# adaLN shift and scale made 128 features at a time with stationary weights, and the first projections of token tile 0 accumulated k-outer

## The chip, the cores and the metric

The kernel runs on all 8 cores of one Trainium2 chip, one batch element per core, with no traffic between the cores. The metric is the device time of the slowest core, in microseconds. Some executions here fell in a second, slower state, in which the cores of a die show a lower granted TensorE clock: in two slow runs of the kernel before (3706.1 and 3710.7 us) one die had 0.81. In the fast profile of the kernel before, all 8 cores were granted 1.00 in the MLP stretch (2000 to 2200 us), with PE busy 199 us or more. A profile is one execution, and the page shows its slowest core. Where I give medians over the cores, I read the same landmark on all 8 cores of the profiled execution.

## The reference, cut to what matters

```python
cond = jax.nn.silu(c)
mod = cond @ w_mod[l] + b_mod[l]                      # (B, 6D), D = 2048
sh_a, sc_a, gt_a, sh_m, sc_m, gt_m = split(mod, 6)
h = rmsnorm(x, g_pre_mix[l]) * (1.0 + sc_a) + sh_a    # (B, S, D), S = 2048
proj = h @ w_in[l]                                    # q, k, v, forget gate, ...
log_f = log_sigmoid(fg + b_forget)                    # then a cumulative sum over S
# ... forgetting attention, sliding-window attention, out projection, MLP ...
```

Only the opening is at issue: shift `sh_a` and scale `sc_a`, `h`, and the first projections (q and k of head 0, v of heads 0 and 1, and the forget gate). Nothing can be projected before the shift and scale are known, and those need 33.5 MB of fp32 weights per core.

## The kernel before: the parts that matter

Tokens are handled in 4 tiles of 512 (`t`), features in 16 groups of 128 (`k`). x lies transposed: features on partitions. Every operation names what it reads and writes; a small scheduler adds the semaphore waits. Each engine is given its own operations in program order. Weights are loaded by the POOL queue with a cast from fp32 to bf16; x and small tensors are loaded by the SP queue.

```python
R1 = Ring(P, "ra", [B[f"ring{i}"] for i in range(5)], src1, ...)   # 5 slots of 128 x 2048

def mod_slot(g, k):          # feature group k of c stationary (32 columns), 4 x 512 weights moving
    s = R1.acq(("M", g, k)); b = R1.bufs[s]
    mms = [mm(banks[MB](0, 512, p=(32*c, 32*c+32)), condpad(k), b(slice(c*512, c*512+512)), k == 0, k == KC-1)
           for c in range(4)]
    ...                      # R1.rel(s) then asks for the next slot
def mod_finish(g, pend): ... # copy to SBUF, select and transpose with 4 fp32 matmuls, add the bias

def n_stat(t, q):            # squares of 4 feature groups on ACT, summed over features by PE
    act(sqA(), x(slice(4*q, 4*q+4)), AF.Square)
    bk = banks[SB[t % 2]]
    pe([mm(bk(), ones(), sqA(i), ...) for i in range(4)], [ones(), sqA()], [bk()])
def n_z(t, k):               # x * scale * rstd, on DVE, in place
    stt(x(k), x(k), Av(0, slice(k, k+1)), rstd[t % 2](), ALU.mult, ALU.mult)
def n_h(t, k):               # + shift, to bf16
    if k % 2 == 0: act(hT(t, k), x(k), AF.Identity, bias=modT(slice(k, k+1)))
    else:          ts(hT(t, k), x(k), modT(slice(k, k+1)), ALU.add, eng="pool")

for k in range(KC):
    mod_slot(1, k)                                  # scale: 16 slots
    if k in (8, 10, 12, 14): n_stat(0, (k-8)//2)
n_rstd(0); mod_finish(1, pend0); x_load(1, extra=[o_sc]); pend0.pop(0)()
for k in range(KC):
    mod_slot(0, k); n_z(0, k)                       # shift: 16 slots
    if k in (12, 13, 14, 15): n_stat(1, k-12)
n_rstd(1); mod_finish(0, pend0); pend0.pop(0)()
for k in range(KC): n_h(0, k)
# [cut] q0, k0, v0 weights acquired from R1
for t in range(NT):          # q, k, forget gate, v of tile t; between their groups, for tile t+1:
    # n_stat x4 (t+1 >= 2), n_rstd, then n_z and n_h for 16 k; then x_load(t+2)
    ...
    fg_tr(t)                 # PE transposes of the gate's running sum; the next tile's projections follow
```

## Time and profile before

| what (core 0, the slowest) | us |
|---|---|
| whole time, median of 3 runs | 3192.5 |
| modulation weights on their way | 1.6 to about 128 |
| h of tile 0 made | 141 to 163 |
| forget-gate scan of tiles 0, 1, 2, 3 starts | 175.5, 212.4, 248.0, 267.8 |
| first forgetting-attention subtraction | 284.3 |
| everything after it | 2911 |

The four scans are good landmarks: each follows the forget-gate projection of its tile.

First the windows view of the kernel before. Each line is a stretch of 20 us: length, then the busy time and instruction count of PE, PE's weight loads, DVE, ACT and POOL, then the granted TensorE clock, the DMA engines' busy share, and GB/s.

```profile
60.00:80.00 20.00, 9.18 (x40) 3.48 (x40) 5.90 (x11) 4.37 (x4) 3.17 (x6) 0.50 1.04 189
100.00:120.00 20.00, 3.71 (x24) 0.84 (x24) 0.00 (x0) 0.00 (x0) 3.17 (x6) 0.50 1.05 178
140.00:160.00 20.00, 4.40 (x12) 1.45 (x11) 9.89 (x17) 7.38 (x12) 18.86 (x7) 0.50 0.27 46
160.00:180.00 20.00, 18.47 (x96) 9.82 (x98) 4.38 (x5) 5.06 (x8) 15.24 (x10) 0.78 0.04 9
```

In 60:80 and 100:120 the DMA engines are full and no other engine is busy half of the time. (GB/s counts what lands; the weights halve on landing, a slot of 1.049 MB landing as 512 KB, so the 178 GB/s that landed in 100:120, nearly all of it weights, are about 345 GB/s read.) From 140 to 160 us the DMA engines are nearly done, PE works 4.4 of 20 us, and POOL is busy for 18.9 us.

The timeline of the kernel before, DVE and POOL around that stretch (start, duration, engine, line, operation, destination and source, count, and the idle time before it with what ended it):

```profile
141.14 21.79 POOL L415 TENSOR_SCALAR hT<-xst_50,modT 128x512 bf16<-128x512 f32 x8 [4.36 <-DVE modT L404]
141.50 9.22 DVE L409 SCALAR_TENSOR_TENSOR xstA<-xstA,Av,rstd_81 128x512 f32<-128x512 f32 x14
175.54 1.21 DVE L696 TENSOR_TENSOR_SCAN Cf<-rr,lf 8x512 f32<-8x512 f32 x1 [2.16 <-ACT lf L401]
```

POOL takes 21.8 us for eight additions, and PE waits for them (17.4 us in 5 waits, from 0 to 290 us). What this line hides is in the tile view of the same POOL operations, which gives the shortest, median and longest of the eight in ns:

```profile
L415 POOL TENSOR_SCALAR hT<-xst_50,modT x8: 1552/1552/11010, 141.1 to 161.4; 128x512 bf16<-128x512 f32 x8
```

One takes 11.0 us, the others 1.55 us. The long one is the first, at 141.1 us, and it ends 1.4 us after DVE's run of 14 back-to-back multiplications beside it.

### The profile page before, as it was taken

The page shows a single profiled execution, that of the slowest core. Times are in us where ns is not written, and L with a number is a line of the kernel's source. Part 1 is how long each engine was busy: PE and PEld are TensorE (multiplying, and loading weights), DVE is VectorE, ACT ScalarE, POOL GpSimd, SP SyncE. Part 2 cuts the span into 40 slices and gives each one's busy share as a digit, 9 for nine tenths or more (in the row PEclk, how much of TensorE's full clock was granted, in tenths as well). Part 3 has the DMA queues.
Part 4 walks back from the last instruction along what each step waited for, and adds up shares of the span by engine and source line. Part 5 has one row for each costly group of instructions (what it writes and reads, how often), then busy time and mean ns, then how long its engine had stood idle before and what let it go on. Part 6 is the DMA issues. An engine that isn't in the chain of part 4 may idle for free.

```text
span 3195.4 us, 36955 instructions; the slowest of 8 cores (3178.6 to 3195.4 us)
## 1 busy us (share of the span) xinstructions
PE 2873.5 (90%) x13961; PEld 1359.6 (43%) x14224; DVE 876.0 (27%) x1344; ACT 757.9 (24%) x1228; POOL 585.2 (18%) x682
## 2 busy tenths in 40 slices
PE   2278988998888898999999999999999999999994
PEld 0034533666433343344444444444444444444441
DVE  0223334244444455643111100000133211000005
ACT  1142233264445434533111100000111111000000
POOL 1342133100000155530000011111100000111114
PEclk8578999999999998999999999999999999999997
DMA  9834545522333833354444455555688644444455
GB/s 190 162 106 90 86 80 83 93 50 55 67 65 76 139 106 119 139 132 70 75 79 74 79 94 97 97 95 90 139 186 194 116 73 79 74 78 76 76 95 201
DMA packets 99199, 325.71 MB, mean 102 GB/s; under 512 B 12080, under 2 KB 12208, under 8 KB 92624
## 3 DMA queue, kind: packets, MB, share of 16 engines
q0 software_dynamic: 58320, 211.87, 39.9%
q1 hardware_dynamic: 40704, 111.46, 10.2%
q8 instruction: 115, 1.88, 0.2%
q14 instruction: 60, 0.49, 0.1%
HBM read 493.12 MB, written 42.01 MB: 167 GB/s over the span
## 4 chain that ended last, share of the span: by engine, by line
PE 79%; DVE 5%; issue 5%; DMA 4%; ACT 4%; POOL 3%; DVEq 0%; POOLq 0%; ACTq 0%; SPq 0%
PE bank L384 79%; DMA ring_70<-w_mod 4%; DVE bank L404 2%; POOL qrot L404 1%; ACT qrot L401 1%; POOL acc_188 L404 1%; DVE bank L409 1%; DVE xstA L409 1%; ACT rr L401 1%; ACT sqA L401 1%; DVE mixF L409 1%; DMA cfb_80<-crow 0%; DMA xstA<-xP 0%; POOL hT L415 0%; DVE mix L404 0%
## 5 line engine op out<-in xcount | busy, mean ns | idle before, releaser
L415 DVE TENSOR_SCALAR bank<-bank 128x512 f32<-128x512 f32 x256 | 166.1, 695 | 646.7 <-PE bank L384 624.5
L418 DVE COPY mixF<-bank 128x512 f32<-128x512 f32 x64 | 41.3, 687 | 842.8 <-PE bank L384 790.1
L401 ACT ACTIVATE sq_185<-bank 128x512 f32<-128x512 f32 x59 | 35.2, 597 | 827.5 <-DVE mixF L418 792.9
L384 PE MATMUL bank<-mix,rung_111 128*128 128x512 bf16 x1002 | 226.4, 381 | 1.1
L384 PE MATMUL bank<-mix,rung_110 128*128 128x512 bf16 x1004 | 225.2, 379 | 1.1
L384 PE MATMUL bank<-mix,rung_113 128*128 128x512 bf16 x1004 | 225.0, 379 | 1.1
L384 PE MATMUL bank<-mix,rung_112 128*128 128x512 bf16 x1004 | 224.9, 379 | 1.1
L404 DVE TENSOR_TENSOR bank<-bank,cfb_82 128x512 f32<-128x512 f32 x192 | 119.3, 630 | 127.0 <-PE bank L384 121.8
L384 PEld LDWEIGHTS bank<-mix,rung_111 128*128 128x128 bf16 x1024 | 100.5, 98 | 123.6 <-issue 4.0
L384 PEld LDWEIGHTS bank<-mix,rung_110 128*128 128x128 bf16 x1024 | 100.4, 98 | 120.7
L384 PEld LDWEIGHTS bank<-mix,rung_113 128*128 128x128 bf16 x1024 | 100.3, 98 | 120.7
L384 PEld LDWEIGHTS bank<-mix,rung_112 128*128 128x128 bf16 x1024 | 100.0, 98 | 121.3 <-issue 0.6
L384 PE MATMUL bank<-hT,ring_71 128*128 128x512 bf16 x566 | 142.7, 382 | 3.1 <-DVE mix L404 2.2
L384 PE MATMUL bank<-hT,ring_69 128*128 128x512 bf16 x436 | 117.5, 406 | 27.7 <-POOL hT L415 17.4
L404 POOL TENSOR_TENSOR acc_187<-acc_187,sq_185 128x512 f32<-128x512 f32 x59 | 74.7, 1266 | 122.4 <-ACT sq_185 L401 122.4
L404 DVE TENSOR_TENSOR bank<-bank,cfb_80 128x512 f32<-128x512 f32 (+3 forms) x128 | 74.1, 596 | 83.6 <-PE bank L384 73.0
L384 PE MATMUL bank<-hT,ring_68 128*128 128x512 bf16 x312 | 79.0, 388 | 4.3 <-DVE mix L404 3.1
L404 POOL TENSOR_TENSOR acc_188<-acc_188,sq_186 128x512 f32<-128x512 f32 x59 | 74.4, 1262 | 45.2 <-ACT sq_186 L401 43.0
L384 PEld LDWEIGHTS bank<-hT,ring_71 128*128 128x128 bf16 x576 | 54.9, 98 | 63.2 <-issue 7.4
L384 PE MATMUL bank<-qT_72,kT_73 128*128 128x512 bf16 (+3 forms) x151 | 52.7, 349 | 32.3 <-ACT Pb_87 L401 20.0
L384 PEld LDWEIGHTS bank<-hT,ring_69 128*128 128x128 bf16 x448 | 43.9, 102 | 85.4 <-issue 46.6
L404 POOL TENSOR_TENSOR qrot<-qrot,sinT 128x512 f32<-128x512 f32 x40 | 50.4, 1260 | 128.1 <-ACT qrot L401 128.1
(643 smaller groups left out, 4722.3 us busy)
## 6 DMA issues: line engine op xcount, KB each, us to landing
rung_110<-wU POOLq DMA_DIRECT2D x32, 512.0 KB, 5.9
rung_111<-wU POOLq DMA_DIRECT2D x32, 512.0 KB, 6.0
rung_112<-wU POOLq DMA_DIRECT2D x32, 512.0 KB, 5.8
rung_113<-wU POOLq DMA_DIRECT2D x32, 512.0 KB, 5.9
rung_110<-wD POOLq DMA_DIRECT2D x32, 512.0 KB, 6.0
rung_111<-wD POOLq DMA_DIRECT2D x32, 512.0 KB, 5.8
rung_112<-wD POOLq DMA_DIRECT2D x32, 512.0 KB, 6.1
rung_113<-wD POOLq DMA_DIRECT2D x32, 512.0 KB, 6.4
```

Source lines behind the costliest of these rows:

```text
L384: ins = e.matmul(o, lhsT=l, rhs=rh, start=st, stop=sp)
L401: return P.op("act", lambda e: e.activation(out=out.ap, in_=in_.ap, func=func, **kw), r, [out])
L404: return P.op(eng, lambda e: e.tensor_tensor(out=out.ap, in0=a.ap, in1=b.ap, op=op), [a, b], [out])
L409: return P.op("dve", lambda e: e.scalar_tensor_tensor(out=out.ap, in0=a.ap, scalar=sc, in1=b.ap, op0=op0, op1=op1), r, [out])
L415: return P.op(eng, lambda e: e.tensor_scalar(out=out.ap, in0=a.ap, scalar1=sc, scalar2=None, op0=op), r, [out])
L418: return P.op("dve", lambda e: e.tensor_copy(out=out.ap, in_=a.ap), [a], [out])
```

## The change

The intent is to use the 125 us in which DMA sets the pace. The weights for shift and scale are laid out so that one slot holds all 2048 inputs of 128 features (`wMA`). They become the stationary operand, and the moving operand is one column of c, so after two slots the shift and scale of one feature group are done (`chunk`). That group of h can be made at once, and the projections of tile 0 can accumulate it (`wave0`, k as the outer loop), all while later weights arrive. The ring for these slots has 6 buffers of its own. Two more parts ride along: `n_h` moves from POOL to ACT (three of four) and DVE (one of four), and x has two alternating buffers.

```diff
-    xst0, xstA = B["xst0"], B["xstA"]
+    xst = [B["xstA"], B["xstB"]]
+    RM = Ring(P, "rm", [B[f"rmod{i}"] for i in range(NRM)], lambda key: dram(T["wMA"][key[0], key[1]]), orders.get("rm"))
     def n_h(t, k):
-        if k % 2 == 0:
+        if k % 4 == 3:
+            ts(hT(t, k), x(k), modT(slice(k, k + 1)), ALU.add)
+        else:
             act(hT(t, k), x(k), AF.Identity, bias=modT(slice(k, k + 1)))
-        else:
-            ts(hT(t, k), x(k), modT(slice(k, k + 1)), ALU.add, eng="pool")
     [cut: the bias negation and a memset stay here, now ahead of the loop below]
+    def chunk(m):
+        bk = banks[6 + m % 2]
+        for g in (1, 0):
+            s = RM.acq((g, m))
+            ...
+            pe([mm(bk(g, g + 1), b(slice(k * 128, k * 128 + 128)), c.re(condpad.h[:, k, 0:1]), k == 0, k == KC - 1)
+                for k in range(KC)], [b(), c], [bk()])
+            RM.rel(s)
+        ... # add the bias to both columns, make Av
+    for m in range(KC):
+        chunk(m)
+        if m == 2:
+            R1.start()                       # the five projection weights
+            W["q"] = sq0 = R1.acq(("A", I_Q))
+            ...
+        if m in (1, 2, 3):
+            for q in ((0,), (1, 2), (3,))[m - 1]:
+                n_stat(0, q)
+        if m == 3:
+            n_rstd(0)
+            ...                              # n_z and n_h for k = 0, 1, 2
+        if m >= 3:
+            n_z(0, m)
+            n_h(0, m)
+        if m == 10:
+            x_load(1, extra=[None if dry else P.ops[-1]])
+        if m in (12, 13, 14, 15):
+            n_stat(1, m - 12)
+        if m >= 7:
+            for _ in range(3 if m < 12 else 1):
+                if done < m:
+                    wave0(done)
+                    done += 1
+    while done < KC:
+        wave0(done)
+        done += 1
+    n_rstd(1)
+    x_load(2)
+    ... # evacuate q, k, v of tile 0
+    for k in range(KC):
+        n_z(1, k)
+        n_h(1, k)
+    fg_post(0, banks[SB[0]])
+    fg_tr(0)
-    for t in range(NT):
+    for t in range(1, NT):
```

More of the change, by code (lines that the diff above doesn't have):

```diff
@@ L26 @@
 NRB = 4
+NRM = 6
 ENG_ATTR = {"pe": "tensor", "act": "scalar", "dve": "vector", "pool": "gpsimd", "sp": "sync"}
@@ L425, in src1 @@
         _, g, k = key
-        return dram(T["w_mod"][k * 128:(k + 1) * 128, g * 2048:(g + 1) * 2048])
+        return dram(T["wMB"][k * 128:(k + 1) * 128, (g - 2) * 2048:(g - 1) * 2048])
     R1 = Ring(P, "ra", [B[f"ring{i}"] for i in range(5)], src1, orders.get("r1"))
+    RM = Ring(P, "rm", [B[f"rmod{i}"] for i in range(NRM)], lambda key: dram(T["wMA"][key[0], key[1]]), orders.get("rm"))
     def src2(key):
@@ L442, in program @@
     dma("sp", sel4(), dram(T["k_sel4"]), "s_s4")
-    R1.start()
+    RM.start()
     for q in range(4):
-        dma("sp", xst0(slice(4 * q, 4 * q + 4)), dram(T["xP"][0][:, 4 * q:4 * q + 4, :]), f"xs{q}")
+        dma("sp", xst[0](slice(4 * q, 4 * q + 4)), dram(T["xP"][0][:, 4 * q:4 * q + 4, :]), f"xs{q}")
     dma("sp", bfg(p=(0, 8)), dram(T["b_fg"]), "s_bf")
@@ L501, in xs_of @@
     def xs_of(t):
-        return xst0 if t == 0 else xstA
+        return xst[t % 2]
     def x_load(t, extra=()):
         for q in range(4):
-            dma("sp", xstA(slice(4 * q, 4 * q + 4)), dram(T["xP"][t][:, 4 * q:4 * q + 4, :]), f"xa{q}", extra=extra)
+            dma("sp", xs_of(t)(slice(4 * q, 4 * q + 4)), dram(T["xP"][t][:, 4 * q:4 * q + 4, :]), f"xa{q}", extra=extra)
     def n_stat(t, q):
@@ L659, in program, with fg_mm, fg_post @@
     F = Fill()
-    pend0 = []
-    for k in range(KC):
-        mod_slot(1, k)
-        if k in (8, 10, 12, 14):
-            n_stat(0, (k - 8) // 2)
-    n_rstd(0)
-    mod_finish(1, pend0)
-    o_sc = None if dry else P.ops[-1]
-    x_load(1, extra=[o_sc])
-    pend0.pop(0)()
-    for k in range(KC):
-        mod_slot(0, k)
-        n_z(0, k)
-        if k in (12, 13, 14, 15):
-            n_stat(1, k - 12)
-    n_rstd(1)
-    mod_finish(0, pend0)
-    pend0.pop(0)()
-    for k in range(KC):
-        n_h(0, k)
+    def fg_mm(t, k, bk):
+        pe([mm(bk(p=(0, 8)), wfg(slice(k * 8, k * 8 + 8)), hT(t, k), k == 0, k == KC - 1)], [wfg(), hT(t, k)], [bk()])
     def fg(t):
         bk = next_pj()
+        for k in range(KC):
+            fg_mm(t, k, bk)
+        fg_post(t, bk)
+    def fg_post(t, bk):
         sl = slice(t * TS, t * TS + TS)
-        pe([mm(bk(p=(0, 8)), wfg(slice(k * 8, k * 8 + 8)), hT(t, k), k == 0, k == KC - 1) for k in range(KC)],
-           [wfg(), hT(t)], [bk()])
         act(lf(sl, p=(0, 8)), bk(p=(0, 8)), AF.Exp, bias=bfg(slice(1, 2), p=(0, 8)), scale=-1.0)
@@ L710, in program @@
     P.op("dve", lambda e: e.memset(rr.h[0:8, :], 1.0), [], [rr()])
-    sq0 = R1.acq(("A", I_Q))
-    sk0 = R1.acq(("A", I_K))
-    sv0 = [R1.acq(("A", I_V)), R1.acq(("A", I_V + 1))]
+    def chunk(m):
+        bk = banks[6 + m % 2]
+        for g in (1, 0):
+            s = RM.acq((g, m))
+            b = RM.bufs[s]
+            c = condpad()
+            pe([mm(bk(g, g + 1), b(slice(k * 128, k * 128 + 128)), c.re(condpad.h[:, k, 0:1]), k == 0, k == KC - 1)
+                for k in range(KC)], [b(), c], [bk()])
+            RM.rel(s)
+        for g in (1, 0):
+            c = g * 16 + m
+            tt(modT(slice(c, c + 1)), bk(g, g + 1), bmod(slice(c, c + 1)), ALU.add)
+        stt(Av(0, slice(m, m + 1)), modT(slice(16 + m, 17 + m)), 1.0, gv(0, slice(m, m + 1)), ALU.add, ALU.mult)
@@ new lines, in program, with wave0 @@
+    W = {}
+    def wave0(k):
+        h = hT(0, k)
+        for i, key in enumerate("qk"):
+            b = R1.bufs[W[key]]
+            pe([mm(banks[PJ[i]](), b(slice(k * 128, k * 128 + 128)), h, k == 0, k == KC - 1)], [b(), h], [banks[PJ[i]]()])
+        b = R1.bufs[W["v"][k // 8]]
+        kk = k % 8
+        for i in range(2):
+            ob = banks[OB[i]]
+            pe([mm(ob(bi * 256, bi * 256 + 256), hT(0, k, slice((2 * i + bi) * 128, (2 * i + bi) * 128 + 128)),
+                   b(slice(kk * 256, kk * 256 + 256)), k == 0 and bi == 0, k == KC - 1 and bi == 1) for bi in range(2)], [b(), h], [ob()])
+        fg_mm(0, k, banks[SB[0]])
@@ new lines, in program @@
+    done = 0
+    for m in range(KC):
[3 more added lines that the diff above has]
+            W["q"] = sq0 = R1.acq(("A", I_Q))
+            W["k"] = sk0 = R1.acq(("A", I_K))
+            W["v"] = sv0 = [R1.acq(("A", I_V)), R1.acq(("A", I_V + 1))]
+        if m in (1, 2, 3):
[3 more added lines that the diff above has]
+            n_rstd(0)
+            for k in range(3):
+                n_z(0, k)
+                n_h(0, k)
+        if m >= 3:
[10 more added lines that the diff above has]
+                    done += 1
@@ L717, in chunks @@
+    while done < KC:
[3 more added lines that the diff above has]
+    x_load(2)
+    ev_q(0)(0)(banks[PJ[0]])
+    ev_k(0)(0)(banks[PJ[1]])
+    for i in range(2):
+        src = banks[OB[i]]()
+        cp(vX(slice(2 * i, 2 * i + 2)), src.re(src.ap.rearrange("p (a d) -> p a d", a=2)))
+    for k in range(KC):
+        n_z(1, k)
+        n_h(1, k)
+    fg_post(0, banks[SB[0]])
+    fg_tr(0)
     def chunks(lst, n):
@@ L1147, in program @@
         P.emit()
-    return {"r1": R1.used, "r2": R2.used}
+    return {"r1": R1.used, "r2": R2.used, "rm": RM.used}
 def build():
@@ L1160, in build @@
     din("c_col", [128, KC])
-    din("w_mod", [D, 6 * D])
+    din("wMA", [2, KC, 128, 2048])
+    din("wMB", [D, 4 * D])
     din("b_modT", [128, 96])
@@ L1196, in build @@
     buf("hT", H, [NT, KC, TS], BF16)
-    buf("xst0", H + 32768, [16, TS], F32)
+    buf("xstB", MIX + 32768, [16, TS], F32)
     for i in range(16):
@@ L1212, in build @@
         o = buf(f"cfb{i}", o, [TS], F32)
+    for i in range(NRM):
+        buf(f"rmod{i}", o + 16384 - 4096 * (i + 1) if i < 4 else o - 4096 * (i - 1), [2048], BF16)
     for nm in ("qT1", "kT1"):
@@ L1277, in _host_inputs @@
     shared = {
-        "w_mod": np.ascontiguousarray(g["w_mod"][0]),
+        "wMA": np.ascontiguousarray(g["w_mod"][0][:, :4096].reshape(16, 128, 2, 16, 128).transpose(2, 3, 1, 0, 4).reshape(2, 16, 128, 2048)),
+        "wMB": np.ascontiguousarray(g["w_mod"][0][:, 4096:]),
         "b_modT": np.ascontiguousarray(g["b_mod"][0].reshape(96, 128).T),
```

## The prediction

> **What bounds the kernel now.** Only the opening 284 of 3192 us are touched; from the first forgetting-attention subtraction (DVE, 284.28 us in the timeline) on, both kernels do the same work, PE-bound (79% of the chain of waits).
>
> - 3 to 128 us: DMA. Its share is about 1.0 from 20 to 140 us (windows view); PE waits 98 us for ring loads of w_mod (tile view). 32 slots of 1.05 MB fp32 plus 8.4 MB of x must arrive; undisturbed slots come 3.07 us apart (109.3 to 124.7 us): 341 GB/s read. [...]
> - 141 to 163 us: h of tile 0. POOL takes 21.8 us for its 8 additions, ACT 5 us for its 8; PE waits for POOL, three short groups apart.
> - Projections: the forget-gate scans of tiles 0 to 3 start at 175.5, 212.4, 248.0, 267.8 us. The 36 us periods are not PE work (about 18 us) but a chain: x load after the scan, four squares at 4 us each through one buffer (1.9 us ACT, 1.9 us PE at granted clock 0.5), 1.3 us rstd, 16 DVE multiplications of 0.66 to 0.8 us.
>
> **Removed:** POOL's additions; the 32-column mod matmuls, their copy and selector matmuls (3 us on the chain); tile 0's projections after h; one x load's wait.
>
> **Added:** 512 one-column matmuls with a 128x128 weight load each. LDWEIGHTS of that size average 98 ns: I estimate 3.2 us per 128 features (two slots, at least 6.1 us of DMA): hidden. Tile 0's waves (18 us, perhaps twice that at clock 0.5) hide there too. DVE gets 4 additions per tile.
>
> **Moved:** five projection-weight slots, loaded at 122 to 150 us before, now load amid the modulation stream: 5.2 MB, so 15 us onto the DMA-bound part. The last chunk lands at about 143 us (47.6 MB at 340 GB/s, plus 3.3 us), not 128. That gives back much of the gain.
>
> **Sum (estimates from the durations above).** Last wave ends at about 148 us. Then tile 1's normalization runs with PE nearly idle: 2 us evacuations, 16 multiplications and 4 additions on DVE (12.6 us), then the gate and its scan, after them in program order: scan 0 at about 164 us (-11.5). To scan 1 about 31 us: x of tile 2 is already there, 6 us less. To scan 2 about 35 us: the x load still follows scan 1 in the sync queue, and DVE still limits. To scan 3 about 19.5 us. Scan 3 at about 249.5 us against 267.8: 18 us gained, all on the critical path, kept to the end because nothing later changes.
>
> **Prediction: 3174 us (-0.6%), 8 in 10 between 3155 and 3190 us.** Faster by over 2%: 0.03; within 2%: 0.95; slower by over 2%: 0.02.
>
> **What would show each step.** Right: DMA share near 1.0 until about 143 us; last one-column matmul at 141 to 147 us; scans at about 164, 195, 230, 249; first subtraction at about 266 us; unchanged durations after it. Wrong: one-column matmuls well above 100 ns a pair; DMA share dropping during the waves; last chunk well before 140 us.
>
> **What would make it wrong.** PE at half clock: [...] the trace grants 0.5 from 60 to 160 us. With three waves per chunk, PE could need over 6 us per chunk and starve the six-slot ring (+5 to 15 us). [...]

(267.8 - 249.5 is about 18 us gained, 3192 - 18 = 3174 us. "Perhaps twice that at clock 0.5" agrees with the trace of before, core 0: 128x512 matmuls in unbroken succession start every 0.22 us at granted clock 1.00 (2050 to 2054 us) and every 0.43 us at 0.50 (154 to 164 us).)

## The result, and the profile after

| fast runs | before | changed |
|---|---|---|
| runs (us) | 3192.06, 3192.5, 3195.86 | 3195.01, 3195.69, 3195.86 |
| ratio, 95% interval | | 1.0006 (0.9984 to 1.0029) |

A ratio is the mean time of one kernel's fast runs over that of the other's of the same rounds, so it is not quite the ratio of the medians I quote. One run of each kernel fell in the slow state (3369.4 and 3367.2 us) and is left out. The time did not move; I had predicted 18 us less.

The landmarks, as medians over the 8 cores of the profiled execution, put the loss in one place:

| us from the start | before | changed | predicted |
|---|---|---|---|
| last matmul of the modulation | 134.6 | 157.8 | 141 to 147 |
| scan of tile 0 | 174.4 | 178.2 | 164 |
| scan of tile 1 | 210.2 | 207.7 | 195 |
| scan of tile 2 | 245.0 | 243.1 | 230 |
| scan of tile 3 | 264.0 | 264.2 | 249 |
| first subtraction | 280.7 | 281.4 | 266 |
| from there to the end | 2906.9 | 2911.2 | unchanged |

(The "last matmul" of before is its last slot's; the selector matmuls follow. "Predicted" stands beside core 0 of before, which is some 4 us later than the median at scan 3, so I had also measured my gain from a late core.) The distances between the scans are nearly as predicted. Nearly the whole error is in the first line: the modulation ends some 14 us later than the middle of the range predicted.

The windows view of the changed kernel, same stretches and columns:

```profile
60.00:80.00 20.00, 0.57 (x16) 0.51 (x16) 0.91 (x2) 0.72 (x1) 1.06 (x2) 1.00 1.04 173
100.00:120.00 20.00, 11.42 (x126) 5.80 (x124) 3.89 (x13) 1.44 (x2) 3.18 (x6) 0.69 1.04 198
140.00:160.00 20.00, 11.04 (x88) 5.18 (x90) 1.88 (x8) 4.54 (x4) 0.00 (x0) 0.50 0.74 192
160.00:180.00 20.00, 3.80 (x15) 1.57 (x14) 16.18 (x26) 12.13 (x18) 0.00 (x0) 0.67 0.16 52
```

The DMA share is 1.04 in the first two lines and still 0.74 in 140:160. The dead stretch for PE (3.8 of 20 us) has moved from 140:160 to 160:180, where DVE and ACT now make tile 1's h.

The timeline of the changed kernel, PE and DVE at the end of the stream (core 4, the slowest):

```profile
140.26 1.86 PE L385 MATMUL bank<-sqA,ones 128*128 128x512 bf16 x4 [4.22 <-ACT sqA L402]
153.54 1.48 PE L385 MATMUL bank<-sqA,ones 128*128 128x512 bf16 x3 [4.60 <-ACT sqA L402]
158.37 0.57 PE L385 MATMUL bank<-condpad,rmod_84 128*128 128x1 bf16 x16 [0.60 <-DMA rmod_84<-wMA]
163.58 0.38 PE L385 MATMUL bank<-hT,wfg 128*8 128x512 bf16 x1
179.13 1.21 DVE L683 TENSOR_TENSOR_SCAN Cf<-rr,lf 8x512 f32<-8x512 f32 x1 [0.95 <-ACT lf L402]
180.49 0.56 PE L691 MATMUL bank<-identF,Cf 8*128 8x8 f32 x4 [16.52 <-DVE Cf L683]
```

The last modulation slot arrives only just before 158.4 us, 0.6 us after PE was ready for it. The last wave of tile 0 runs at 163.6 us, and then PE idles 16.5 us until the scan is done. Earlier, PE also waited over 4 us for a square on ACT, again and again.

Why do the bytes come so late? The SP and POOL queues in the timeline of the changed kernel:

```profile
108.89 2.55 SPq L207 DMA_DIRECT2D xstB<-xP  x4
120.36 41.04 SPq L207 DMA_DIRECT2D xstA<-xP  x4
124.86 0.53 POOL L207 DMA_DIRECT2D rmod_84<-wMA  x1 [6.18 <-PE bank L385]
```

The second line is four issues in one. In narrower windows the second and the third of them stand alone:

```profile
126.31 0.33 SPq L207 DMA_DIRECT2D xstA<-xP  x1
132.45 0.33 SPq L207 DMA_DIRECT2D xstA<-xP  x1
```

This is the load of tile 2's x: in program order it stands after the whole loop, but on the SP queue nothing holds it back. A quarter of the buffer is free as soon as tile 0's h of those four groups is made. So three of its four quarters are issued during the stream, at 120.4, 126.3 and 132.5 us; only the fourth comes after it, at 161.1 us. The last modulation slot is issued at 124.9 us, on the other queue, and takes 33.4 us to land; the quarters take at most 25.2 us, so all three land before it, although two of them were issued after it. The two queues share the engines: from 120 to 140 us SP's queue held 51% of them and POOL's 50%. I had read the order of the queue and overlooked that its position in the program does not delay it. (The expectation of the first experiment puts all three quarters at 120 us; only the first is that early.)

Some of PE's waits from 0 to 290 us in the kernel before and in the changed one (what was waited for: us in total, times, longest; among those left out are more waits for weights, and one for ACT's Pb of 11.6 and 13.4 us):

```profile
PE bank L384 <- ACT sqA L401: 19.5, 11, 3.2
PE bank L384 <- POOL hT L415: 17.4, 5, 13.4
```

```profile
PE bank L385 <- DMA rmod_83<-wMA: 29.2, 3, 17.5
PE bank L385 <- ACT sqA L402: 28.8, 12, 4.7
PE bank L691 <- DVE Cf L683: 16.5, 1, 16.5
PE bank L385 <- DVE modT L405: 11.8, 1, 11.8
```

The wait for POOL is gone. In its place there are three candidates: a wait for the scan (16.5 us), more time behind the squares, and one of 11.8 us early on. The last comes from a tiny load of the forget-gate bias. It is issued on the SP queue at 6.0 us, after the four quarters of tile 0's x, the last of which is issued at 5.2 us and takes 33.1 us to land; DVE can read the bias at 38.6 us (core 4). DVE waits for it, and the additions that free a bank for PE come after it in DVE's program order. A list of waits does not tell which of these cost anything. The runs do.

### The profile page after: what moved, and what is told of

Same layout as the page of the kernel before. It is cut to its first block, busy times and chain, and to the rows that moved or that the text cites. A ratio compares the mean times of both kernels' runs of the same rounds, so it can differ in the third digit from the quotient of the medians.

```text
span 3194.3 us, 37768 instructions; the slowest of 8 cores (3185.7 to 3194.3 us)
## 1 busy us (share of the span) xinstructions
PE 2866.9 (90%) x14323; PEld 1367.1 (43%) x14592; DVE 886.2 (28%) x1403; ACT 769.4 (24%) x1244; POOL 519.2 (16%) x650
## 4 chain that ended last, share of the span: by engine, by line
PE 79%; DVE 5%; DMA 5%; issue 4%; ACT 4%; POOL 2%; SPq 0%; DVEq 0%; POOLq 0%; ACTq 0%
PE bank L385 79%; DMA rmod_84<-wMA 3%; DVE bank L405 1%; POOL qrot L405 1%; ACT qrot L402 1%; DMA bfg<-b_fg 1%; POOL acc_194 L405 1%; DVE bank L410 1%; ACT rr L402 1%; DVE mixF L410 1%; DVE xstB L410 1%; ACT sqA L402 0%; DMA cfb_80<-crow 0%; DVE mix L405 0%; ACT Pb_97 L402 0%
## 5 line engine op out<-in xcount | busy, mean ns | idle before, releaser
L402 ACT ACTIVATE sq_191<-bank 128x512 f32<-128x512 f32 x59 | 35.2, 597 | 827.1 <-DVE mixF L419 793.0
L385 PE MATMUL bank<-qT_72,kT_73 128*128 128x512 bf16 (+3 forms) x151 | 52.7, 349 | 34.0 <-ACT Pb_93 L402 21.8
L385 PE MATMUL bank<-qT_89,kT_90 128*128 128x512 bf16 (+3 forms) x154 | 55.0, 359 | 21.2 <-ACT Pb_93 L402 7.5
```

The lines of the kernel that those rows point to most:

```text
L385: ins = e.matmul(o, lhsT=l, rhs=rh, start=st, stop=sp)
L402: return P.op("act", lambda e: e.activation(out=out.ap, in_=in_.ap, func=func, **kw), r, [out])
```

## The experiments

My theory: the stream is bound by bytes, and the bytes are in the wrong order; the waits on the scan and on the bias are shadows. Rivals: the bias wait, or the wait for the scan, or the streamed form as such. All runs gave correct results. Run labels beginning with `a` are edits of the changed kernel, those with `b` edits of the kernel before.

| run | fast runs: median us (count) | ratio to before | last modulation matmul | scans 0, 1, 2, 3 | first subtraction |
|---|---|---|---|---|---|
| before | 3192.5 (3) | | 134.6 | 174.4, 210.2, 245.0, 264.0 | 280.7 |
| changed | 3195.7 (3) | 1.0006 | 157.8 | 178.2, 207.7, 243.1, 264.2 | 281.4 |
| a_hold_x2 | 3191.4 (4) | 0.9998 | 152.4 | 172.0, 201.5, 236.4, 257.4 | 274.2 |
| a_bias_late | 3197.8 (3) | 1.0016 | 157.6 | 178.1, 207.5, 242.4, 263.6 | 281.1 |
| a_gate_first | 3197.7 (5) | 1.0047 | 158.4 | 165.3, 208.1, 243.2, 264.5 | 280.8 |
| b_no_pool | 3179.2 (2) | 0.9959 | 134.3 | 157.4, 192.9, 227.8, 248.2 | 264.5 |
| a_sq_early | 3193.9 (3) | 1.0021 | 157.6 | 177.3, 206.6, 241.2, 262.1 | 279.0 |
| a_hold_sq_early | 3188.0 (4) | 0.9999 | 150.0 | 170.2, 198.5, 234.3, 254.1 | 272.2 |
| b_no_pool_x2buf | 3177.7 (3) | 0.9976 | 133.5 | 156.8, 192.0, 226.8, 247.4 | 263.7 |
| a_x1_first | 3172.1 (5) | 0.9932 | 148.3 | 155.2, 184.1, 219.7, 240.0 | 255.8 |
| a_x1_all | 3165.4 (4) | 0.9914 | 149.1 | 155.9, 182.8, 211.3, 231.9 | 247.6 |
| b_all3 | 3169.0 (4) | 0.9925 | 133.1 | 154.0, 183.8, 218.2, 237.5 | 253.4 |
| a_x1_weights_last | 3190.3 (1) | | 135.8 | 172.3, 200.6, 235.4, 256.2 | 272.5 |
| b_dve_waits | 3190.4 (2) | | 133.7 | 165.6, 201.9, 237.0, 256.1 | 271.6 |

Landmarks are medians over 8 cores of one profiled execution. In three of the profiled runs that count as fast, one pair of cores took some 20 us longer (3213.0 us among the three of a_sq_early, for instance). The loss lies far behind the opening: in a_sq_early, cores 6 and 7 were granted 0.79 to 0.81 of the clock from 1300 to 1400 us, the other six 0.90 to 1.00 (means over the whole run 0.956, and 0.963 to 0.966; spans 3211 us, and 3186 to 3192). In a_x1_first it was cores 4 and 5, with 0.79 to 0.81 in the same stretch (means 0.960 and 0.962, the others 0.969 to 0.971; 3189 us, and 3163 to 3171). These runs widen the intervals and pull the ratios up, so for effects under 0.5% I go by the landmarks and the medians.

### Hold tile 2's x back until the last chunk

```diff
-    x_load(2)
+    x_load(2, extra=[o_mod])      # o_mod: the last operation of the last chunk
```

> The changed kernel, with one more dependency: the load of tile 2's x may not start before the last modulation chunk has been added up. Theory (bytes in the wrong order: in the changed kernel three quarters of tile 2's x, 3.1 MB, are issued at 120 us, ahead of the last modulation slots, and at about 335 GB/s cost 9 us): the last one-column matmul moves from 159 us to about 150 us, the forget-gate scan of tile 0 from 179 to about 170 us, the first subtraction from 283 to about 274 us, the whole time falls by about 9 us (0.3%). Rival (the stall of 12 us that the tiny bias load puts on DVE and then on PE at 26 to 39 us delays the whole ring): the last matmul stays at 157 to 159 us and the time does not move.

Measured: the last modulation matmul came at 152.4 us instead of 157.8, all scans 6 to 7 us earlier, the first subtraction 7 us earlier. The median time was 3191.4 us against 3195.7 for the changed kernel on another chip, and against 3197.8 on the same chip for a_bias_late, whose landmarks are the changed kernel's. The direction is the theory's; the size is about two thirds of the 9 us expected. The trace says why. In this run the last two chunks no longer waited for their loads (PE timeline, core 7, the lines between left out):

```profile
143.44 0.97 PE L385 MATMUL bank<-condpad,rmod 128*128 128x1 bf16 x32
148.63 1.86 PE L385 MATMUL bank<-sqA,ones 128*128 128x512 bf16 x4 [4.22 <-ACT sqA L402]
152.65 1.01 PE L385 MATMUL bank<-condpad,rmod 128*128 128x1 bf16 x32
```

Both slots of a chunk (x32) run at once with no wait before them; the 4.2 us are spent ahead of the squares' sum. The square of tile 1 stands on ACT behind h of the chunk's own features, so each chunk pays in turn: chunk, scale, h, square, sum, wave. A second limit had lain right behind the bytes.

### Move the bias out of DVE's way

```diff
-    ts(bfg(slice(1, 2), p=(0, 8)), bfg(slice(0, 1), p=(0, 8)), -1.0, ALU.mult)
-    P.op("dve", lambda e: e.memset(rr.h[0:8, :], 1.0), [], [rr()])
     ...                           # the loop over chunks, and the waves
+    ts(bfg(slice(1, 2), p=(0, 8)), bfg(slice(0, 1), p=(0, 8)), -1.0, ALU.mult)
+    P.op("dve", lambda e: e.memset(rr.h[0:8, :], 1.0), [], [rr()])
     n_rstd(1)
```

> The changed kernel, with the forget-gate bias negation (which waits for a tiny load until 38.6 us) and the memset after it moved behind the waves, so that the first chunk's additions on DVE do not stand behind it. Theory (the modulation stage is bound by bytes, and the ring still has four slots outstanding during the stall): PE no longer waits from 26 to 39 us, the weight slots of the projections are asked for earlier, but the last one-column matmul stays within 2 us of 159 us, scan 0 within 2 us of 179, and the time within 3 us of the changed kernel. Rival (the stall delays the ring): the last matmul at about 147 us and the time 10 to 12 us lower.

Measured: last modulation matmul 157.6 us (157.8 without the edit), scan 0 at 178.1 (178.2). The rival falls. PE's early wait cost nothing, because the ring had slots outstanding all along and the DMA engines never ran dry (share 1.03 from 20 to 40 us in the changed kernel).

### The gate of tile 0 before tile 1's normalization

```diff
+    fg_post(0, banks[SB[0]])
+    fg_tr(0)
     for k in range(KC):
         n_z(1, k)
         n_h(1, k)
-    fg_post(0, banks[SB[0]])
-    fg_tr(0)
```

> The changed kernel, with the forget gate of tile 0 and its transposes put before tile 1's normalization in program order. Theory (PE's longest wait in this stretch, 16.5 us for scan 0, is not what bounds: the squares of tile 2 on ACT follow tile 1's additions in either order): scan 0 comes at about 166 us instead of 179, PE starts tile 1's first projection some 10 us earlier, but the first square of tile 2 starts within 2 us of 179 us, the scan of tile 1 within 3 us of 208.6, and the time within 3 us of the changed kernel. Rival (this wait is where the expected gain went): scans 1, 2 and 3 all move up by 10 us or more, and the time falls by as much.

Measured: scan 0 moved from 178.2 to 165.3 us, and nothing else moved: scan 1 at 208.1 (207.7), scan 3 at 264.5 (264.2). The longest single wait of PE after the stream was a shadow. ACT makes tile 1's h and only then squares tile 2, and that order did not change. The ratio of 1.0047 contains fast runs of 3210.8 and 3223.0 us; the other three lie at 3195.2 to 3197.7.

### The kernel before, with h off POOL and nothing else

```diff
-        if k % 2 == 0:
+        if k % 4 == 3:
+            ts(hT(t, k), x(k), modT(slice(k, k + 1)), ALU.add)
+        else:
             act(hT(t, k), x(k), AF.Identity, bias=modT(slice(k, k + 1)))
-        else:
-            ts(hT(t, k), x(k), modT(slice(k, k + 1)), ALU.add, eng="pool")
```

> The kernel before, with one part of the change alone: the additions that make h move from POOL to ACT (three of four) and DVE (one of four). No streaming of the modulation, no waves, no second x buffer. Theory (POOL's 22 us were the only part of tile 0's stretch that the change had to remove): PE starts tile 0's projections at about 145 us instead of 154 with no waits on POOL, scan 0 comes at about 163 us instead of 175.5, the first subtraction at about 272 us instead of 284, and the time falls by about 12 us (0.4%), more than the whole change gains. Rival (the streaming is what carries the change's gain, and POOL's work is hidden elsewhere): the time stays within 3 us of the kernel before.

Measured: scan 0 at 157.4 us instead of 174.4, first subtraction 264.5 instead of 280.7, and 3178.5 and 3179.8 us in its two fast runs (ratio 0.9959, interval 0.9939 to 0.9979). This smallest part of the change gains 16 us on the landmarks by itself, more than the 12 us expected. So the rest of the change, the streamed form with its second x buffer, takes about 17 us back: 264.5 against 281.4 us at the first subtraction.

### Squares ahead of the chunk, without and with the hold

```diff
     for m in range(KC):
+        if m in (12, 13, 14, 15):
+            n_stat(1, m - 12)
         chunk(m)
     ...
-        if m in (12, 13, 14, 15):
-            n_stat(1, m - 12)
```

> The changed kernel, with the squares and sums of tile 1's statistics put ahead of the modulation chunk instead of behind that chunk's h on ACT; the load of tile 2's x is left where it was. Theory (two limits lie one behind the other: bytes, 51.5 MB of reads before the last slot at about 332 GB/s, and a chain chunk, scale, h, square, sum that makes PE wait 4.2 us for ACT in each of chunks 12 to 14): PE's waits for the square before chunks 13 to 15 go away, but the bytes still end at about 158 us, so the last one-column matmul comes at 156 to 159 us, scan 0 at 176 to 179 and the time stays within 3 us of the changed kernel. Rival (the chain alone bounds the tail): the last matmul at 147 to 150 us and 8 to 10 us off the time.

> Both edits together: tile 2's x held back until the last chunk, and tile 1's squares ahead of the chunk. Theory (with x held back the chain is what bounds: in the run with the hold alone, the last two chunks lay ready and PE waited 4.2 us for ACT before each): the last one-column matmul at about 147 us (47.6 MB at 332 GB/s after 3.3 us) against 152 with the hold alone and 158 in the changed kernel, scan 0 at about 167 us, the first subtraction at about 268 to 271 us, 10 to 12 us off the changed kernel's time. Rival (the rate of loads while two queues share the engines falls to 320 GB/s, and that is why the hold gave 6 us and not 9): the last matmul stays at 151 to 152 us.

Measured: alone, the last modulation matmul stayed at 157.6 us, as the theory of two limits one behind the other has it. With the hold it came at 150.0 us, against 152.4 with the hold alone. I had expected 147, and 151 to 152 if a lower load rate were to blame; 150.0 lies between, so this run does not decide between the two. PE still waited about 2 us for each square, since the sum now waits for ACT to finish the chunk before. The first subtraction came at 272.2 us, 9 us before the changed kernel's, and the time was 3188.0 us (median of 4, with one run of 3207.1 in it).

### The kernel before with h off POOL and two x buffers

```diff
-    xst0, xstA = B["xst0"], B["xstA"]
+    xst = [B["xstA"], B["xstB"]]
     for k in range(KC):
         n_h(0, k)
+    x_load(2)
     ...
-        if t + 2 < NT:
+        if 0 < t and t + 2 < NT:
             jobs += [lambda: x_load(t + 2)]
```

> The kernel before with two parts of the change, still without the streamed modulation: h on ACT and DVE instead of POOL, and x in two alternating buffers, the load of tile 2's x issued as soon as tile 0's h is made. Theory: scan 0 as with the first part alone (157 us), scan 1 about 5 us earlier than with the first part alone (188 us against 193), as x of tile 2 no longer starts after scan 0; scans 2 and 3 keep their distance (35.5 and 20.5 us), as tile 3's x still starts after scan 1. About 5 us off the time of the first part alone, about 21 us (0.7%) off the kernel before. If the second buffer were worthless: the same as the first part alone, 17 us off.

Measured: scan 1 at 192.0 us against 192.9 with the first part alone; I had expected 188. A miss. The load was no longer waited for, but the first square of tile 2 started at 164.2 us on core 0, where it had started at 165.5 with the first part alone, because ACT was making the last of tile 1's h until then, itself waiting for DVE's multiplications. The wait for the load had become a wait for tile 1's h. The second buffer is worth about 1 us here.

### Tile 1's x first, its h beside tile 0's

```diff
+    for q in range(4):            # directly after the small loads at the start
+        dma("sp", xst[1](slice(4 * q, 4 * q + 4)), dram(T["xP"][1][:, 4 * q:4 * q + 4, :]), f"xa{q}")
     for m in range(KC):
+        if m == 6:
+            for q in range(4):
+                n_stat(1, q)
+            n_rstd(1)
-        chunk(m)
+        o_mod = chunk(m)
     ...
-        if m == 10:
-            x_load(1, extra=[None if dry else P.ops[-1]])
-        if m in (12, 13, 14, 15):
-            n_stat(1, m - 12)
+        if m == 6:
+            for k in range(6):
+                n_z(1, k)
+                n_h(1, k)
+        if m >= 6:
+            n_z(1, m)
+            n_h(1, m)
     ...
-    n_rstd(1)
-    x_load(2)
+    x_load(2, extra=[o_mod])
     ...
-    for k in range(KC):
-        n_z(1, k)
-        n_h(1, k)
```

> The changed kernel with the hold, and with tile 1's x loaded directly after tile 0's, its statistics ahead of chunk 6, and its h made chunk by chunk beside tile 0's: the bytes are the same, only their order and the place of the work change. Theory (the streamed form loses because tile 1's normalization, 13 us of DVE, and tile 0's gate come after the last chunk with PE idle): last one-column matmul at about 147 to 149 us, scan 0 at about 152 us instead of 179, PE without its wait of 16.5 us, scan 1 at about 183 us, scan 2 about 218, scan 3 about 240, first subtraction about 257 us; about 25 us off the changed kernel and 0.8% off the kernel before. Rival (the streamed modulation itself costs more than it can hide): scan 3 at 250 us or later, no better than the first part alone on the kernel before.

Measured: last modulation matmul 148.3 us, scans at 155.2, 184.1, 219.7 and 240.0, first subtraction at 255.8 us, 3172.1 us (ratio 0.9932, interval 0.9916 to 0.9949). Every landmark is within 3.2 us of what was written down; the time fell by 0.7%, not 0.8%. The bytes are those of the hold. The rival, that the streamed form costs more than it can hide, falls: 26 us before the changed kernel and 9 us before the kernel with the first part alone.

### The version the runs point to, and its counterpart without the stream

On top of the previous run: the bias out of the way, tile 3's x asked for directly after the waves, and the squares in halves.

```diff
-        act(sqA(), x(slice(4 * q, 4 * q + 4)), AF.Square)
         bk = banks[SB[t % 2]]
-        pe([mm(bk(), ones(), sqA(i), q == 0 and i == 0, q == 3 and i == 3) for i in range(4)], [ones(), sqA()], [bk()])
+        for j in (0, 2):
+            sq2 = sqA(slice(j, j + 2))
+            act(sq2, x(slice(4 * q + j, 4 * q + j + 2)), AF.Square)
+            pe([mm(bk(), ones(), sqA(i), q == 0 and i == 0, q == 3 and i == 3) for i in (j, j + 1)], [ones(), sq2], [bk()])
```

> The version that the runs so far point to: the changed kernel with the hold, tile 1's x first and its h beside tile 0's (as in the run before), and three more edits: the bias negation moved out of the way, the squares taken in halves through two half buffers, so that ACT squares one half while PE sums the other, and tile 3's x asked for as soon as its buffer is free instead of after scan 1. Theory (the distance between scans is a chain of four squares at 4 us, rstd and 16 multiplications, not PE work): the squares take about 9.5 us instead of 16, so scan 0 stays at 154, scan 1 at about 177 us (183 to 186 without), scan 2 at about 203 (216 to 222 without), scan 3 about 224, first subtraction about 239 to 242 us, about 15 us off that version and about 1.1% off the kernel before. Rival (DVE's multiplications or PE's work bound the distance): the distances stay at 29.5 and 35 us.

> The kernel before with h on ACT and DVE, two x buffers and the squares in halves, without the streamed modulation. Theory: scan 0 as before with the first part (157 us, perhaps 2 us less as tile 1's squares shorten too), each distance to the next scan about 6 us shorter than the 35.5 us without the halves, scan 3 at about 236 us, first subtraction about 252 us; about 0.9% off the kernel before, and some 8 to 12 us behind the best streamed version. If the streamed form were worthless once its order is mended, this one would be level with it or ahead.

Measured: a_x1_all took 3165.4 us (ratio 0.9914, interval 0.9901 to 0.9928) and is the fastest version, below both kernels. The gain over the run before it was 8 us at the first subtraction (247.6 against 255.8), not 15. Scan 1 came at 182.8 us where I expected 177. Its chain of waits on core 5 shows what took over (start, duration, what the chain passed through):

```profile
151.89 0.50 DVE hT L416
152.46 15.49 DMA xstA<-xP
168.08 1.07 ACT sqA L402
```

Tile 2's x now arrives last. It may start only after the last chunk, and 15.5 us pass until its last part has landed. Bytes bound again. Tile 3's x is asked for at the same time; what that adds to the 15.5 us is not shown. The distance from scan 1 to scan 2, where no load is waited for, fell from 35.6 to 28.5 us; that edit bundles halves and early load, and only the counterpart below parts them.

The counterpart b_all3 (the kernel before with h off POOL, two x buffers and squares in halves) took 3169.0 us, ratio 0.9925. The two ran on the same chip in the same rounds, and all four fast runs of a_x1_all (3165.1 to 3166.1 us) lie below all four of b_all3 (3169.0 to 3171.3): about 4 us, or 0.1%, where I had expected 8 to 12. But this is not shown to be the worth of the stream, because b_all3 lacks one more edit: the early load of tile 3's x. At scan 1 a_x1_all is only 1.0 us ahead (182.8 against 183.8); from scan 1 to scan 2 it needs 28.5 us and b_all3 34.4, and this makes up the whole 5.8 us at the first subtraction (247.6 against 253.4). In that stretch b_all3's squares wait for just that load (timeline of ACT, core 0, the line between left out):

```profile
192.79 2.00 ACT L401 ACTIVATE sqA<-xstB 128x1024 bf16<-128x1024 f32 x2 [2.83 <-DMA xstB<-xP]
200.42 2.00 ACT L401 ACTIVATE sqA<-xstB 128x1024 bf16<-128x1024 f32 x2 [1.91 <-DMA xstB<-xP]
```

So the halves gain where x has already landed (scan 0 to scan 1: 29.8 us, against 35.2 without halves in b_no_pool_x2buf) and next to nothing where it is still landing (scan 1 to scan 2: 34.4 against 34.8). A kernel without the stream but with that early load was not run; a lead of the stream over it is not shown.

### What the moved bytes cost

A test of one term, not a candidate. On a_x1_first, the five projection weights are asked for after chunk 12, and all waves follow the last chunk.

```diff
-        if m == 2:
+        if m == 12:
             R1.start()
-        if m >= 7:
+        if m >= KC:
             for _ in range(3 if m < 12 else 1):
```

> The version with tile 1's x first, with the five projection weights asked for only when all modulation slots have been issued (after chunk 12 instead of chunk 2), and all waves of tile 0 after the last chunk. A test of what the moved bytes cost, not meant to be fast. Theory (bytes set the last chunk): 5.2 MB at 332 GB/s are 15.8 us, so the last one-column matmul moves from 148 or 149 us to 132 or 134 us, where the kernel before has it; scan 0 then waits for the weights and for 16 waves and comes later, at 170 to 176 us instead of 154. Rival (the one-column form itself, or its layout, loads more slowly than the kernel before): the last matmul stays well above 135 us.

Measured: the last modulation matmul moved from 148.3 to 135.8 us (133.2 to 137.0 over the cores), 12.5 us for 5.2 MB, and scan 0 moved out to 172.3 us. The kernel before has its last slot at 134.6. The 135.8 us are a little later than the 132 to 134 expected, but not "well above 135", as the rival has it. The one-column form and the contiguous layout therefore load no more slowly; the five weights are most of what puts the streamed form's last chunk late. The run does not isolate their bytes: the waves move too, and the weights now follow the last modulation slot, so the DMA engines stay full until it has landed (share 1.03 to 1.11 from 130 to 138 us on core 0; more on this below).

### Why one POOL addition took 11 us

The kernel before, with one wait added:

```diff
     for k in range(KC):
-        n_h(0, k)
+        o_h = n_h(0, k)
+    P.op("dve", None, extra=[o_h])     # DVE waits here for POOL's last addition
```

> The kernel before, POOL's additions kept, with one wait added: DVE does not start tile 1's multiplications until POOL has made the last of tile 0's h. In the trace of before the first of POOL's 8 additions lasted 11.0 us, from 141.1 to 152.2 us, just through DVE's run of 14 back-to-back multiplications (141.5 to 150.7 us), the other seven 1.55 us each. Theory ([...] the cost is the neighbour, not POOL's own speed): all 8 additions take about 1.55 us, h of tile 0 is ready at about 153.5 us instead of 163, scan 0 comes 8 to 9.5 us earlier (165 to 167 us, against 174.4 in the median of before's cores), scans 1 to 3 move by 5 to 9 us, and the time falls by 5 to 9 us, about half of what taking the additions off POOL gave. Rival (the first addition is long for a reason of POOL's own, such as its first use after DMA issues): the first addition stays at 11 us and, as DVE now waits for it, the time does not fall.

Measured, tile view of POOL's additions, core 0 (shortest, median, longest in ns; the first line is tiles 1 to 3, the second tile 0):

```profile
L415 POOL TENSOR_SCALAR hT<-xstA,modT x24: 1555/1681/9222, 155.0 to 245.4; 128x512 bf16<-128x512 f32 x24
L415 POOL TENSOR_SCALAR hT<-xst,modT x8: 1552/1552/1558, 140.4 to 151.2; 128x512 bf16<-128x512 f32 x8
```

All eight of tile 0 now take 1.55 us. The long one has moved to tile 1: 9.2 us, from 155.0 us on, where DVE's run of 14 multiplications now is (153.5 us, for 9.23 us); it ends 1.4 us after the run, as the long one did before. Scan 0 came at 165.6 us instead of 174.4, and the first subtraction at 271.6 instead of 280.7. The times do not settle it (two fast runs, 3187.7 and 3193.1 us, no interval), the landmarks do: the cost of POOL was its neighbour. Beside DVE's 14 back-to-back multiplications one addition took 11.0 and 9.2 us, without them 1.55 us. By what mechanism is not shown (a clause of the expectation about it is cut). Nor did it help to be first: in the kernel before, by the recorded starts, POOL's long addition began 0.35 us before DVE's run on all 8 cores (POOL's recorded times are rough).

## Why the prediction was wrong

- **Where it failed.** The step was "The last chunk lands at about 143 us (47.6 MB at 340 GB/s, plus 3.3 us), not 128." Measured: about 158 us. Two terms were wrong in it.
  - *The bytes.* Three quarters of tile 2's x, 3.1 MB, landed ahead of the last slot, because the load was held back by its buffer and its queue, not by its place in the program (issued at 120.4, 126.3 and 132.5 us, 38 to 26 us before the last chunk's matmul at 158.4). Holding it back gave 5.4 us by itself, and 7.8 us together with the mended order of the squares.
  - *The rate.* 37 slots of 1.049 MB, 11.5 MB of x and 0.2 MB of small tensors are 50.5 MB by 158.2 us, which is 326 GB/s from 3.3 us on. In a_x1_first it was 47.4 MB by 147.6 us, 328 GB/s. (The 51.5 MB in an expectation above are about one quarter of x more; that quarter was issued only at 161 us.) I took 340 from an undisturbed stretch of the kernel before. At a mean of 327 GB/s the 47.6 MB of the prediction end at 149 us, and 50.5 MB at 158. But the rate of the full engines was not the error: from 20 to 150 us the changed kernel read 43.9 MB (17.35 MB landed from the POOL queue, read as twice that, and 9.20 MB from SP's), which is 338 GB/s. The mean is lower because of the two ends. In the first 20 us the DMA share is 0.86, and in the last microseconds the engines are mostly empty while the last slot is still on its way (windows view, core 4; the DMA share is the last column but one):

```profile
152.00:154.00 2.00, 0.46 (x2) 0.32 (x4) 0.00 (x0) 1.01 (x1) 0.00 (x0) 0.50 0.87 260
154.00:156.00 2.00, 2.00 (x7) 0.81 (x6) 0.00 (x0) 0.59 (x1) 0.00 (x0) 0.50 0.39 125
156.00:158.00 2.00, 1.77 (x21) 0.77 (x19) 0.00 (x0) 1.32 (x1) 0.00 (x0) 0.50 0.11 27
```

The kernel before does not pay the second end, because five more slots follow its last modulation slot (share 1.04 in 120:140). Why the last slot lands so late behind the others was not tested and stays open.

- **A limit I did not see at all**: PE's waits for the square in chunks 12 to 14. Behind the bytes it cost nothing in the changed kernel (a_sq_early), but it halted the gain when the bytes were mended (a_hold_x2, then a_hold_sq_early).
- **Right: the direction of the moved weights.** "That gives back much of the gain" held, with 12.5 us measured against 15 estimated (a_x1_weights_last).
- **Right: everything after the last chunk.** From the last matmul to scan 0: 20.4 us measured, 19 to 21 in the prediction's sum. To scan 1 29.5 us (31 predicted), to scan 2 35.4 (35), to scan 3 21.1 (19.5), to the first subtraction 17.2 (16.5).
- **Wrong in size, without effect: the one-column matmuls.** I estimated 3.2 us per 128 features; 16 pairs of a 128x128 weight load and a one-column matmul take 0.57 us, about 36 ns a pair, so 1.1 us for the two slots. PE never starved the ring; it waited 77.6 us for the slots (0 to 290 us, core 4).
- **Half right: POOL's additions.** They were the critical work, but I read 21.8 us as eight slow operations. It was seven of 1.55 us and one of 11.0 us, beside DVE's run of multiplications. Mending that pair in the kernel before gained 9 us (b_dve_waits) and 16 us (b_no_pool) at the first subtraction.
- **Not explained.** From the first subtraction to the end the changed kernel needs 2911.2 us in the median of its cores, the kernel before 2906.9. Most streamed variants show 2911, the variants without the stream 2908 to 2910. I have not traced these 2 to 4 us. They are part of why the gain at the landmarks shows smaller in the times.

So the expected gain was real where it was expected (h off POOL, 16 us), and the streamed modulation gave all of it back by ending some 23 us later than before (134.6 to 157.8 us; only some 18 us if one compares when DVE adds the bias to the last of the modulation, 140.3 and 158.5 us in the median of the cores, since the selector matmuls of before still follow its last slot), with tile 1's 13 us of normalization still to come after it. Ordered so that tile 1 rides along, the same stream, together with h off POOL, gains 0.7%; h off POOL alone gains 0.4%.

## What to carry to other kernels

When a stage is bound by loads, write down which bytes must have landed before its last step, and then check for each load what really holds it back; here it was its buffer and its queue, not its place in the program. Work that is hidden under a stream only pays if what follows the stream becomes shorter too, so move along whatever else depends on the streamed data. And look at the longest of a group of instructions beside its mean: here eight operations of 2.7 us were seven of 1.55 and one of 11.0 beside a busy neighbour.
